# The inverse of a head pair one step earlier in the trace, and three kinds of staging tiles ahead of the merge

## The chip, the cores and the metric

The kernel runs on one core of one Trainium2 chip. The metric is device time in microseconds: the median of three runs is 2133.5 us (2132.93, 2133.5 and 2137.12). A profile is one more execution, taken by the hardware profiler.

## What is computed

One layer of a hybrid encoder on 1024 frames of width 1024, and a final RMSNorm. Cut to what the change touches:

```python
# per head (8 of 128 columns) and chunk, q, k, v after a causal convolution and SiLU
lower = where(strict, beta[..., None] * (k @ k.T) * decay, 0)
sol = triangular_solve(lower, rhs, unit_diagonal=True)     # rhs = [beta*v, beta*exp(gc)*k]
delta = u - w @ state                                      # over the chunks, one after another
o = q_dec @ state + a_qk @ delta
state = g_end * state + k_dec.T @ delta
# then: rmsnorm(o)*silu(z) @ w_branch_gdn, a second branch (GLA) @ w_branch_gla, both merged by gates
```

The rest (GLA branch, cross attention over 256 memory tokens, a squared-ReLU MLP) stands around it unchanged.

## The kernel before

**Precision and products.** A large product is three matmuls of rounded halves, 128x512 each: high by high (L541), high by low (L543), low by high (L545). The halves come from a split: ScalarE rounds to the high half (L581), VectorE or GpSimd subtracts for the low one (L582). The small products of the delta rule are full fp32; each of them stands as two instructions in the trace.

**The delta rule** works on 4 pairs of heads, each head in 8 chunks of 128 frames. For a pair, `push_keys`, and `push_conv` for q and v, queue projections (`dense`, 48 products of 128x512 for each head's q, k or v, followed by three VectorE convolution steps, L1212). `fill(n)` traces n products from that queue, `until(name)` all up to a name. `gdn_keys` makes the triangular matrix NT (L1273, L1276). `gdn_subst` solves its 32x32 diagonal blocks for both heads at once by 62 dependent steps (L1324, L1326) and transposes the result (L1329, L1333). `gdn_inverse` builds the inverse from these blocks in four stages of small matmuls on TensorE (L1356, L1365, L1372, L1379), each of which waits for an eviction by ScalarE or VectorE (L1357 to L1380). `gdn_scan` runs over the chunks: k S and q S (L1404, L1405), zh (L1407, VectorE), NT zh (L1414), dl (L1416, ScalarE), kdt dl (L1421), the new state S (L1424, L1426, VectorE), and AT dl (L1431) for the output v (L1433, L1435). `gdn_norm` (L1450, GpSimd's power at L572, L573 to L576, L1452), `gdn_out` (L1459) and `gdn_sums` (L1469 to L1474) finish a pair in the next round of the loop.

In a round p of the loop (`phase_gdn`) the trace goes: projections of q and v of pair p and k of pair p + 1 are queued; norm and output of pair p - 1; queries and v of pair p; all queued projections to the end; the inverse of pair p; keys and substitution of pair p + 1; the scan of pair p. In the last round (p = 3) no pair follows: after `drain` the pools of the projections are closed, and `begin_merge` opens those of the merge, whose tiles lie where the projections' weights lay.

**The merge's first products.** `begin_merge` fetches weights of the GLA branch (raw, L501 from in_w_bgla_dram, 512 KB each) and loads 20 blocks of 256 KB (obd) of the GLA output, four for each of five operands, through a staging tile `staged`, and splits each into the operand tiles B0a, B0b, A1a, A1b, A0a. All 20 go through the tile "e", which has 3 buffers. The tiles "q" (4 buffers) and "acc" (2) of the same pool are there for later evictions. The products with these operands (pd<-B0a,wop and so on) come later in the trace than the scan of pair 3.

**What sets the order.** The program is traced twice. In the first pass a planner (`Plan`) records every instruction with its tiles, works out dependences and due times from a table of costs, and schedules each engine's list: among instructions whose inputs it holds to be there, TensorE takes the one that was traced first, the other engines the one due first; some sums may go to VectorE or GpSimd. The second pass fixes each engine's order by it. So a place in the trace is a priority, a later product may fill a gap, and the order on the chip is fixed: an instruction that is late holds up all behind it on its engine. SP issues all large transfers, in its own fixed order.

Of the kernel before, what the change touches and what calls it, by code (L numbers as in the profile page):

```python
# [11 lines left out]
F32 = mybir.dt.float32  # L12
# [6 lines left out]
P = 128  # L19
# [8 lines left out]
HALF = 512  # L28
NEG = -1.0e30
NFILL = 4  # L30
GF = (8, 32, 18, 24, 24, 16, 8)
# [117 lines left out]
class Mark:  # L149

    eng, port, dma, flex, acc, cost, lat, own, opcode = "mark", False, False, False, (), 0, 0, 0, ""
# [311 lines left out]
class Layer:  # L463
# [1023 lines left out]
    def phase_gdn(self, wctx):  # L1487

        nc, a = self.nc, self.a
        with ExitStack() as lctx:  # L1490
# [38 lines left out]
            for p in range(GH // 2):  # L1529
                hs = (2 * p, 2 * p + 1)  # L1530
                for h, st in zip(hs, sts):
                    st["q"] = self.til(sq, [P, NB, P], "q", bufs=2)
                    conv(f"q{h}", h, a["w_gdn"][3 * h + 1], lambda acc, st=st: st["q"])
                for h, st in zip(hs, sts):
                    def out(acc, st=st):
                        st["vT"] = c3(acc)
                        return st["vT"]
                    conv(f"v{h}", 2 * GH + h, a["w_gdn"][3 * h + 2], out)
                nxt = None
                if p < GH // 2 - 1:  # L1540
                    nxt = push_keys((2 * p + 2, 2 * p + 3))
                for _ in range(GN[p]):
                    self.push_gate(next(gates), getw, sp)
                if last:
                    for h, st in last:
                        self.gdn_norm(sv, st)
                    self.fill(GF[1])
                    for h, st in last:
                        self.gdn_out(h, st)
                        self.fill(GF[2])  # L1550
                    self.gdn_sums(p - 1, [st for _, st in last])
                else:
                    PF = keys(hs, sts)
                self.until(f"v{hs[0]}")
                self.gdn_queries(sv, sp, sts[0])
                self.fill(GF[3])
                self.gdn_queries(sv, sp, sts[1])
                self.until(f"v{hs[1]}")
                self.gdn_v(sv, sts[0])
                self.fill(GF[4])  # L1560
                self.gdn_v(sv, sts[1])
                self.fill(GF[5])
                if nxt:
                    self.until(f"k{hs[1] + 2}")
                else:
                    self.drain()
                    ectx.close()
                    wctx.close()
                    ob = self.begin_merge()
                self.gdn_inverse(sts, PF, GF[6])  # L1570
                if nxt:
                    ns = (2 * p + 2, 2 * p + 3)
                    for st, h in zip(nxt, ns):
                        self.load_decay(sp, h, st)
                    PF = keys(ns, nxt)
                self.gdn_scan(sv, sq, hs, sts, NFILL)
                for h, st in zip(hs, sts):
                    self.load_z(sv, h, st)
                last, sts = list(zip(hs, sts)), nxt
            sctx.close()  # L1580
            self.big3(ob)
# [10 lines left out]
    def begin_merge(self):  # L1592
# [8 lines left out]
        self.fetch_w()  # L1601
        ob = {"SL": ("B0a", "B0b", "A1a", "A1b", "A0a", "B1a", "B1b")}
        for p in range(5):
            self.load_op(sp, ob, p, lambda p, k: self.obd[p][:, k], range(4), None)
        return ob

    def big3(self, ob):
# [21 lines left out]
    def staged(self, sp, src, both=True):  # L1629

        self.nraw += 1
        raw = self.til(sp, [P, HALF], "e", bufs=3) if both is None or both and self.nraw % 5 < 3 else \
            self.til(self.lp, [P, HALF], "rawa", bufs=2)
        self.load(raw, src)
        return raw
# [978 lines left out]
```

## Time and profile before

| | |
|---|---|
| median of three runs | 2133.5 us |
| profiled execution | 2135.29 us |
| its span, first to last instruction | 2133.6 us |
| TensorE busy | 2105.5 us, 99% |
| VectorE, ScalarE, GpSimd busy | 79%, 53%, 9% |
| mean granted clock of TensorE | 0.994 |
| inverses of the four pairs begin (L1356) | 701.15, 807.34, 913.45, 1008.93 us |
| substitution of pairs 1, 2, 3: first L1315 to last L1333 starts | 734.48 to 786.49, 840.63 to 892.60, 946.73 to 999.90 us |

Times are in microseconds from the span's start. A row of the timeline has the start, the duration, engine, line, operation, output <- inputs, shape and count, and in brackets the idle time before it with what ended it. Busy time of matmuls is modelled, so what TensorE does in a stretch is better read from the starts of its instructions. A granted clock of 0.50 is half speed.

### The profile page before, as it was taken

To read this page: it belongs to the slowest core of one execution; us is meant where nothing else is said; L and a number is where in the kernel's file an instruction comes from. 1 tells how busy PE (TensorE), PEld (TensorE's weight loads), DVE (VectorE), ACT (ScalarE), POOL (GpSimd) and SP (SyncE) were. 2 spreads that over 40 slices of the span, in tenths; PEclk is the share of its full clock that TensorE was granted. 3 is DMA by queue.
4 is the path that set the end of the run, shared out by engine and by line. 5 is a ranking of instruction groups with operands and counts; after the bars stand their busy time and mean duration, and the time that the engine had idled before them with its cause. 6 is when DMAs were issued, how large, how long until landed. Compare 5 with 4: busy or idle time off the path is not lost.

```text
span 2133.6 us, 31820 instructions
## 1 busy us (share of the span) xinstructions
PE 2105.5 (99%) x11340; PEld 1776.2 (83%) x11340; DVE 1688.6 (79%) x3053; ACT 1127.9 (53%) x2251; POOL 182.2 (9%) x194
## 2 busy tenths in 40 slices
PE   8999999999999999999999999999999999999998
PEld 8789888988888888888888888888888888888887
DVE  7869898779768787877799858789979778577766
ACT  6545554454455656565644446676755556444433
POOL 0001101000001121213000001000201000001011
PEclk9999999999999999999899999999999999999999
DMA  8423333223241030302488664457445546688852
GB/s 306 177 80 111 103 112 128 78 87 123 67 147 60 21 114 21 114 11 83 169 300 293 221 197 131 131 183 246 132 138 160 153 148 186 196 273 278 276 178 94
DMA packets 147040, 321.70 MB, mean 151 GB/s; under 512 B 16056, under 2 KB 19512, under 8 KB 146880
## 3 DMA queue, kind: packets, MB, share of 16 engines
q1 hardware_dynamic: 143984, 315.44, 44.5%
q10 hardware_dynamic: 2896, 4.22, 0.6%
q8 instruction: 89, 1.46, 0.3%
q14 instruction: 71, 0.58, 0.1%
HBM read 223.10 MB, written 96.50 MB: 150 GB/s over the span
## 4 chain that ended last, share of the span: by engine, by line
PE 86%; DVE 7%; DMA 3%; ACT 2%; issue 1%; SPq 0%; DVEq 0%; POOLq 0%; ACTq 0%
PE pd L543 20%; PE pd L541 20%; PE pd L545 20%; PE ps L541 5%; PE ps L545 5%; PE ps L543 5%; PE ps L613 2%; DVE acc L1212 1%; DMA raw<-in_w_dram 1%; DVE wop L582 1%; PE ps L1414 1%; PE ps L1421 1%; PE ps L1431 1%; PE ps L1273 1%; ACT wop L581 1%
## 5 line engine op out<-in xcount | busy, mean ns | idle before, releaser
L581 ACT ACTIVATE wop<-raw 128x512 fp32r<-128x512 f32 (+1 forms) x536 | 358.6, 675 | 560.0 <-PE pd L545 263.3
L582 DVE TENSOR_TENSOR wop<-raw,wop 128x512 fp32r<-128x512 f32 (+1 forms) x506 | 370.1, 735 | 116.4 <-ACT wop L581 109.4
L545 PE MATMUL pd<-A1a,wop 128*128 128x512 f32 x380 | 150.0, 395 | 0.0
L541 PE MATMUL pd<-A1a,wop 128*128 128x512 f32 x380 | 148.9, 392 | 0.0
L543 PE MATMUL pd<-A1b,wop 128*128 128x512 f32 x360 | 141.5, 393 | 0.0
L543 PE MATMUL pd<-A1a,wop 128*128 128x512 f32 x316 | 124.4, 394 | 0.2 <-DVE A1a L582 0.2
L545 PE MATMUL pd<-t,wop 128*128 128x512 f32 x300 | 119.3, 398 | 0.0
L541 PE MATMUL pd<-A1b,wop 128*128 128x512 f32 x296 | 117.4, 397 | 1.5 <-ACT A1b L581 1.5
L541 PE MATMUL pd<-t,wop 128*128 128x512 f32 x300 | 116.9, 390 | 0.4 <-ACT wop L581 0.4
L543 PE MATMUL pd<-t,wop 128*128 128x512 f32 x300 | 117.0, 390 | 0.0
L545 PE MATMUL pd<-A1b,wop 128*128 128x512 f32 x296 | 116.8, 395 | 0.0
L1212 DVE SCALAR_TENSOR_TENSOR acc<-cin,convw,acc 128x1024 f32<-128x1024 f32 x72 | 94.3, 1310 | 25.3 <-ACT acc L1210 24.8
L541 PEld LDWEIGHTS pd<-A1a,wop 128*128 128x128 f32 x380 | 71.6, 188 | 14.5
L545 PEld LDWEIGHTS pd<-A1a,wop 128*128 128x128 f32 x380 | 71.5, 188 | 14.0
L541 PE MATMUL pd<-A0a,wop 128*128 128x512 f32 x200 | 81.2, 406 | 0.0
L543 PE MATMUL pd<-A0a,wop 128*128 128x512 f32 x200 | 79.9, 400 | 0.8 <-DVE A0a L582 0.8
L541 PE MATMUL pd<-B0a,wop 128*128 128x512 f32 x196 | 77.7, 397 | 2.6 <-ACT wop L581 2.0
L545 PE MATMUL pd<-A0a,wop 128*128 128x512 f32 x200 | 79.0, 395 | 0.0
L543 PEld LDWEIGHTS pd<-A1b,wop 128*128 128x128 f32 x360 | 67.9, 188 | 13.1
L545 PE MATMUL pd<-B0a,wop 128*128 128x512 f32 x196 | 77.6, 396 | 0.0
L543 PE MATMUL pd<-A0b,wop 128*128 128x512 f32 x188 | 74.8, 398 | 0.0
L545 PE MATMUL pd<-A0b,wop 128*128 128x512 f32 x188 | 74.3, 395 | 0.0
(646 smaller groups left out, 6027.3 us busy)
## 6 DMA issues: line engine op xcount, KB each, us to landing
raw<-in_w_dram SPq DMA_DIRECT2D x120, 256.0 KB, 3.3
raw<-in_w_dram SPq DMA_DIRECT2D x32, 512.0 KB, 4.2
e<-ad SPq DMA_DIRECT2D x63, 256.0 KB, 3.9
raw<-in_w_gdn_dram SPq DMA_DIRECT2D x24, 512.0 KB, 4.2
ad<-q SPq DMA_DIRECT2D x45, 256.0 KB, 2.9
rawa<-ad SPq DMA_DIRECT2D x42, 256.0 KB, 4.5
A0b<-tgd SPq DMA_DIRECT2D x32, 256.0 KB, 5.2
raw<-in_w_gate_dram SPq DMA_DIRECT2D x15, 512.0 KB, 3.6
```

The source lines that it names most:

```text
L541: nc.tensor.matmul(out, lh, rh, start=first and i == 0, stop=False, skip_group_check=more)
L543: nc.tensor.matmul(out, lh, rl, start=False, stop=False, skip_group_check=more)
L545: nc.tensor.matmul(out, ll, rh, start=False, stop=last and i == n - 1, skip_group_check=more)
L581: nc.scalar.activation(hi, raw, AF.Copy)
L582: (lo_eng or nc.gpsimd).tensor_tensor(lo, raw, hi.bitcast(F32), SUB)
L613: self.nc.tensor.transpose(pt[:, i * P:(i + 1) * P], s, self.ident)
L1212: nc.vector.scalar_tensor_tensor(acc, cin[:, 1 + i:1 + i + T], cw[:, i:i + 1], acc, MUL, ADD)
L1273: nc.tensor.matmul(pt[:, i * P:(i + 1) * P], kc, kc, start=True, stop=True)
L1414: nc.tensor.matmul(py[:, 0:P], st["NT"][:, c, :], zh[h], start=True, stop=True)
L1421: nc.tensor.matmul(pd[h][:, 0:P], st["kd"][:, c, :], dl[h], start=True, stop=True)
L1431: nc.tensor.matmul(po[:, 0:P], st["AT"][:, c, :], dl[h], start=True, stop=True)
```

## The change

Two edits. The call of `gdn_inverse` moves: for pair 0 it follows its substitution at once, and for a later pair it is traced right behind the scan of the pair ahead, at the end of that round, and ahead of the next round's queued projections. And the 20 blocks of the merge's first operands go through the tiles q, acc and e in turn (nine buffers) where they went through e alone (three).

```diff
                 else:
-                    PF = keys(hs, sts)
+                    self.gdn_inverse(sts, keys(hs, sts), GF[6])
...
                     ob = self.begin_merge()
-                self.gdn_inverse(sts, PF, GF[6])
                 if nxt:
...
                     self.load_z(sv, h, st)
+                if nxt:
+                    self.gdn_inverse(nxt, PF, GF[6])
                 last, sts = list(zip(hs, sts)), nxt
...
-            self.load_op(sp, ob, p, lambda p, k: self.obd[p][:, k], range(4), None)
+            self.load_op(sp, ob, p, lambda p, k: self.obd[p][:, k], range(4), 3 if p < 5 else None)
...
-        raw = self.til(sp, [P, HALF], "e", bufs=3) if both is None or both and self.nraw % 5 < 3 else \
+        raw = self.til(sp, [P, HALF], *((("e", F32, 3), ("q", F32, 4), ("acc", F32, 2))[self.nraw % 3])) if both == 3 else \
+            self.til(sp, [P, HALF], "e", bufs=3) if both is None or both and self.nraw % 5 < 3 else \
             self.til(self.lp, [P, HALF], "rawa", bufs=2)
```

The planner makes a new order of it. The first place is on TensorE, at the inverse of pair 3: NT_1682 and NT_1704 are the triangular matrices of its two heads, X_9356 and X_9358 the solved blocks and their transposes, pd the bank of a projection. Before the change, from the last projection products on:

```order
L541 MATMUL pd_10119<-A1a_225,wop_10073 128x512
L543 MATMUL pd_10119<-A1a_225,wop_10073 128x512
L545 MATMUL pd_10119<-A1a_225,wop_10074 128x512
L1356 MATMUL ps_10260<-X_9356,NT_1682_9163 32x32 x16
L1356 MATMUL ps_10279<-X_9356,NT_1704_9229 32x32 x16
L1365 MATMUL ps_10298<-X_9358,X_9356 32x32
L1365 MATMUL ps_10298<-X_9356,X_9358 32x32
L1365 MATMUL ps_10298<-X_9358,X_9356 32x32 x2
```

Before the change these L1356 follow the last projection of the gate, and the rows after them hold no other product. After the change the same place of the program, with the same names for pair 3, reads:

```order
L543 MATMUL pd_10100<-A0b_224,wop_10095 128x512
L1356 MATMUL ps_9650<-X_9356,NT_1682_9163 32x32 x16
L1356 MATMUL ps_9669<-X_9356,NT_1704_9229 32x32 x16
L545 MATMUL pd_10100<-A0b_224,wop_10096 128x512
L541 MATMUL pd_10172<-A1b_5434,wop_10095 128x512
L543 MATMUL pd_10172<-A1b_5434,wop_10095 128x512
L545 MATMUL pd_10172<-A1b_5434,wop_10096 128x512
L541 MATMUL pd_10172<-A1a_225,wop_10095 128x512
L543 MATMUL pd_10172<-A1a_225,wop_10095 128x512
L545 MATMUL pd_10172<-A1a_225,wop_10096 128x512
L541 MATMUL pd_10172<-A1b_5434,wop_10095 128x512
L1365 MATMUL ps_9688<-X_9358,X_9356 32x32
```

What moved: before, pd_10119 was the last projection (the gate's), and the first other product came after L1365 of the second head. Now 40 projection products lie between the scan of pair 2 and this inverse, and 8, 18 and 5 between its steps.

The second place is on TensorE, at the start of the scan of pair 3 (v is that scan's zh, dl and S its delta and state, kdt, AT, k and q its keys and queries; pd_10846 and pd_10861 are the merge's first banks). Before the change, in the scan's first chunk:

```order
L1414 MATMUL ps_10404<-v_10059,NT_1682_9163 128x128
L543 MATMUL pd_10846<-B0a_10175,wop_10796 128x512
L545 MATMUL pd_10846<-B0a_10175,wop_10796 128x512
L1414 MATMUL ps_10408<-v_10102,NT_1704_9229 128x128
L1421 MATMUL ps_10412<-dl_10406,kdt_1663_9116 128x128
L541 MATMUL pd_10846<-B0a_10175,wop_10796 128x512
L543 MATMUL pd_10846<-B0a_10175,wop_10796 128x512
L545 MATMUL pd_10846<-B0a_10175,wop_10796 128x512
L541 MATMUL pd_10861<-B0a_10175,wop_10799 128x512
L1421 MATMUL ps_10416<-dl_10410,kdt_1685_9182 128x128
L1431 MATMUL ps_10420<-dl_10406,AT_9908 128x128
L1431 MATMUL ps_10424<-dl_10410,AT_9981 128x128
```

Here the merge's products with B0a stand between the steps of the chunk. After the change the first chunk reads, with pd_10263 the last projection:

```order
L543 MATMUL pd_10263<-A1a_225,wop_10217 128x512
L545 MATMUL pd_10263<-A1a_225,wop_10218 128x512
L1414 MATMUL ps_10404<-v_10203,NT_1682_9163 128x128
L1414 MATMUL ps_10408<-v_10246,NT_1704_9229 128x128
L1421 MATMUL ps_10412<-dl_10406,kdt_1663_9116 128x128
L1421 MATMUL ps_10416<-dl_10410,kdt_1685_9182 128x128
L1431 MATMUL ps_10420<-dl_10406,AT_10052 128x128
L1431 MATMUL ps_10424<-dl_10410,AT_10125 128x128
L1404 MATMUL ps_10428<-S_10414,k_1569_8541 128x128
L1405 MATMUL ps_10428<-S_10414,q_9792 128x128
L1404 MATMUL ps_10435<-S_10418,k_1570_8542 128x128
L1405 MATMUL ps_10435<-S_10418,q_9793 128x128
```

What moved: now the last projection stands right ahead of the scan, the merge's products are gone from its first five chunks (48 products of the scan follow each other), and 32 of them lie in the rest of it, where 66 lay in the whole scan before.

The third place is on VectorE, at the end of the substitution of pair 1 (pr and Pm are its tiles; L1295 belongs to the queries of pair 1, L573 to L576 and L1452 to the norm of pair 0). Before the change the last steps stand together, behind the queries:

```order
L1295 TENSOR_SCALAR eq_7517<-ssq_7490 128x8
L1324 TENSOR_TENSOR pr_6835<-X_6751,Pm_6753 128x70
L1326 TENSOR_TENSOR Pm_6753<-Pm_6753,pr_6835 128x5x14
L1324 TENSOR_TENSOR pr_6838<-X_6751,Pm_6753 128x56
L1326 TENSOR_TENSOR Pm_6753<-Pm_6753,pr_6838 128x4x14
L1324 TENSOR_TENSOR pr_6841<-X_6751,Pm_6753 128x45
L1326 TENSOR_TENSOR Pm_6753<-Pm_6753,pr_6841 128x3x15
L1324 TENSOR_TENSOR pr_6844<-X_6751,Pm_6753 128x30
L1326 TENSOR_TENSOR Pm_6753<-Pm_6753,pr_6844 128x2x15
L1324 TENSOR_TENSOR pr_6847<-X_6751,Pm_6753 128x16
L1326 TENSOR_TENSOR Pm_6753<-Pm_6753,pr_6847 128x16
L1329 STREAM_TRANSPOSE X_6850<-Pm_6753 128x512
```

In these rows only the steps and the queries meet; the norm of pair 0 lies earlier. After the change the last two steps and the transpose read:

```order
L1324 TENSOR_TENSOR pr_6844<-X_6751,Pm_6753 128x30
L575 TENSOR_SCALAR rs_t_7293<-rs_t_7293 128x8
L574 TENSOR_TENSOR rs_t_7304<-rs_t_7304,vv_7301 128x8
L1326 TENSOR_TENSOR Pm_6753<-Pm_6753,pr_6844 128x2x15
L576 TENSOR_TENSOR rs_o_7294<-rs_y_7292,rs_t_7293 128x8
L1324 TENSOR_TENSOR pr_6847<-X_6751,Pm_6753 128x16
L575 TENSOR_SCALAR rs_t_7304<-rs_t_7304 128x8
L1452 TENSOR_TENSOR v_6446<-v_6446,rs_o_7294 128x1024
L1326 TENSOR_TENSOR Pm_6753<-Pm_6753,pr_6847 128x16
L576 TENSOR_TENSOR rs_o_7305<-rs_y_7303,rs_t_7304 128x8
L1329 STREAM_TRANSPOSE X_6850<-Pm_6753 128x512
L1212 SCALAR_TENSOR_TENSOR acc_7513<-cin_7512,convw_212,acc_7513 128x1024
```

What moved: the end of the substitution has moved ahead of the queries of its pair, in between the steps of the norm of pair 0; in the scan of pair 0 its steps now alternate with those of the scan. Of its 248 steps in the program 49 stood on GpSimd before, none now. On SP nine loads of obd now stand ahead of the four weight loads where three stood, and the first of the nine waits for the last projection product; before, the first of the three waited for none.

## The prediction

> **What bounds the kernel now.** I read the page first. TensorE is busy all along, and the chain that ended last is made of it, so a microsecond counts when TensorE has nothing ready or runs at less than its full clock.
>
> ```profile
> span 2133.6 us, 31820 instructions
> PE 2105.5 (99%) x11340; PEld 1776.2 (83%) x11340; DVE 1688.6 (79%) x3053; ACT 1127.9 (53%) x2251; POOL 182.2 (9%) x194
> PE 86%; DVE 7%; DMA 3%; ACT 2%; issue 1%; SPq 0%; DVEq 0%; POOLq 0%; ACTq 0%
> ```
>
> Work is neither added nor dropped on TensorE; only its order changes. So I looked for stretches in which it loses time, by the windows view. First an inverse in the middle (pair 1), then the last one (pair 3) up to the second chunk of its scan, then one chunk of a scan (pair 0). The columns are length, busy time (count) of PE, PEld, DVE, ACT, POOL, granted clock, DMA.
>
> ```profile
> 807.34:820.86 13.52, 12.87 (x247) 10.66 (x246) 8.29 (x11) 9.07 (x18) 0.10 (x1) 1.00 0.14 41
> 1008.92:1030.03 21.11, 17.58 (x248) 15.54 (x248) 10.11 (x20) 12.61 (x27) 0.00 (x0) 0.60 0.51 176
> 1012.66:1029.73 17.07, 14.60 (x132) 12.84 (x133) 8.89 (x17) 9.22 (x19) 0.00 (x0) 0.50 0.46 172
> 743.74:747.03 3.29, 3.29 (x26) 3.03 (x25) 2.94 (x12) 1.94 (x8) 0.50 (x2) 1.00 0.03 5
> ```
>
> The last inverse and one chunk take 21.11 us with about as many matmuls as the middle one has in 13.52 us, and for 17.07 us the granted clock is 0.50. The timeline of TensorE says why: the last projection product (128x512) starts at 1008.61, and until 1018.06 there is nothing but the small matmuls of the inverse, which wait for their own evictions.
>
> ```profile
> 1008.14 0.40 PE L541 MATMUL pd<-A1a,wop 128*128 128x512 f32 x1
> 1008.38 0.39 PE L543 MATMUL pd<-A1a,wop 128*128 128x512 f32 x1
> 1008.61 0.39 PE L545 MATMUL pd<-A1a,wop 128*128 128x512 f32 x1
> 1008.93 1.81 PE L1356 MATMUL ps<-X,NT 32*32 32x32 f32 x58
> ...
> 1013.17 1.94 PE L1372 MATMUL ps<-subTA,NT 64*64 64x64 f32 x16 [1.54 <-DVE subTA L1366]
> ...
> 1018.06 0.80 PE L541 MATMUL pd<-B0a,wop 128*128 128x512 f32 x1 [1.96 <-ACT wop L581]
> ...
> 1030.03 0.39 PE L1404 MATMUL ps<-S,k 128*128 128x128 f32 x2
> ```
>
> **Part 1: the last inverse gets cover.** In the new order the inverse of pair 3 stands behind the scan of pair 2, where projections are left: 8, 18 and 5 of the 128x512 products lie between its steps. What it costs there I take from pair 1, which has 22 such products inside (247 less the inverse's 224 instructions, less an edge). A 128x512 product holds TensorE 0.23 us (1008.14 to 1008.38 to 1008.61), so pair 1's inverse itself takes 13.52 - 22 x 0.23 = 8.4 us. The last one: 21.1 us, less ten 128x512 products (2.3 us), less the six 128x128 products of the scan's first chunk (1.3 us at 0.22 us each, which the next row block shows): 17.5 us. The cover is worth 17.5 - 8.4 = **9.1 us**.
>
> **Part 2: the scan of pair 3 loses its cover.** With the inverse gone from there, the first five chunks of that scan stand bare: 48 products of 128x128 without one of 128x512 between them. The price comes from one chunk of pair 0, all engines:
>
> ```profile
> 743.74 0.39 PE L1404 MATMUL ps<-S,k 128*128 128x128 f32 x2
> 743.96 0.39 PE L1405 MATMUL ps<-S,q 128*128 128x128 f32 x2
> 744.39 0.35 DVE L1407 SCALAR_TENSOR_TENSOR zh<-ps,geg,v 128x128 f32<-128x128 f32 x1
> 744.87 0.42 PE L1414 MATMUL ps<-zh,NT 128*128 128x128 f32 x2
> 744.87 0.72 ACT L1409 ACTIVATE qs<-ps,geg 128x128 f32<-128x128 f32 x2
> 745.49 0.72 ACT L1416 ACTIVATE dl<-ps,nb 128x128 f32<-128x128 f32 x2
> 746.05 0.70 PE L1421 MATMUL ps<-dl,kdt 128*128 128x128 f32 x4
> 746.47 0.80 DVE L1426 SCALAR_TENSOR_TENSOR S<-S,gge,ps 128x128 f32<-128x128 f32 x2
> ```
>
> A 128x128 product is two instructions, 0.22 us (743.74 to 743.96). A chunk has ten, 2.2 us, and takes 3.29 us; four 128x512 products (0.92 us) fill all but 0.17 us of the rest. The 3.29 us are the chain k S, zh, NT zh, dl, kdt dl, S. Bare, the chunk loses the 0.92 us if the chain keeps its length. ScalarE's new order has the first dl ahead of the second qs, half of 0.72 us earlier: then it is 0.56 us. I take 0.75 us, four times, 3.0 us. The first chunk has only the hops, from start to start, L1414 to L1416 (0.62), to L1421 (0.56), to L1426 (0.42), to L1404 (747.03, 0.56): 2.16 us, less six products, 0.8 us. In the fifth chunk three splits of the staged operands stand on ScalarE ahead of its dl: each takes at least as long as a 128x128 step (0.36 us), 1.1 us in all, and most of it fits into ScalarE's idle time (1.94 of 3.29 us are busy); I add 0.4 us, an estimate. Sum **4.2 us**, between 2.6 (four times 0.56, and 0.4) and 5.6 (four times 0.92, 0.8 and 1.1).
>
> Whether the clock holds there is the second question. What bears on it are stretches of about 3.4 us, three from early in the kernel and two from the last inverse, in the same view as above:
>
> ```profile
> 63.75:67.17 3.42, 2.35 (x9) 1.21 (x8) 3.42 (x7) 0.89 (x2) 0.88 (x1) 1.00 0.02 5
> 67.17:70.58 3.41, 1.16 (x8) 0.97 (x8) 2.16 (x6) 0.81 (x2) 0.00 (x0) 1.00 0.62 192
> 70.58:74.00 3.42, 3.21 (x8) 2.54 (x9) 3.38 (x7) 2.00 (x4) 0.00 (x0) 0.50 0.10 38
> 1009.25:1012.66 3.41, 2.35 (x108) 2.07 (x102) 0.91 (x3) 3.18 (x9) 0.00 (x0) 1.00 0.86 227
> 1012.66:1016.07 3.41, 2.90 (x64) 2.71 (x64) 0.78 (x2) 2.36 (x6) 0.00 (x0) 0.50 0.89 339
> ```
>
> With TensorE busy 2.35 of 3.42 us on whole 128-row products the clock stays at 1.00; after 1.16 of 3.41 us it is 0.50; and after 2.35 of 3.41 us on 32x32 tiles (the row at 1009.25) it is 0.50 as well. The bare scan is busy 2.2 of 3.0 to 3.3 us on whole products, nearest to the first row, so I take no loss. [...]
>
> **Part 3: the substitution gets a date.** The inverse of pairs 1 to 3 now waits for the substitution (L1324, L1326), which VectorE does during the scan ahead; until now it had the whole next round of projections as slack.
>
> ```profile
> 759.60 0.16 DVE L1450 SCALAR_TENSOR_TENSOR vv<-ss,eq 128x8 f32<-128x8 f32 x1
> ...
> 761.55 0.17 DVE L573 TENSOR_TENSOR rs_t<-rs_y 128x8 f32<-128x8 f32 x1 [1.46 <-POOL rs_y L572]
> ...
> 763.16 0.17 DVE L573 TENSOR_TENSOR rs_t<-rs_y 128x8 f32<-128x8 f32 x1 [1.24 <-POOL rs_y L572]
> ...
> 763.64 1.23 DVE L1452 TENSOR_TENSOR v<-v,rs_o 128x1024 f32<-128x1024 f32 x1
> L1324 DVE TENSOR_TENSOR pr<-X,Pm 128x126 f32<-128x126 f32 (+21 forms) x105 | 26.7, 254 | 2.6
> L1326 DVE TENSOR_TENSOR Pm<-Pm,pr 128x110 f32<-128x110 f32 (+13 forms) x94 | 23.7, 252 | 2.4
> L1329 DVE STREAM_TRANSPOSE X<-Pm x4: 1057/1081/1091, 682.8 to 996.1; 128x512 f32<-128x512 f32 x4
> ```
>
> In the new order 12 steps, the norm of the pair ahead and the transpose L1329 stand behind the scan's last v: 12 x 0.25 = 3.0, two waits for GpSimd of some 1.2 = 2.4, L1452 1.2, eight tiny ones some 0.8, L1329 1.1, together 8.5 us and a hop or two. TensorE has 40 products of 0.23 us = 9.2 us before the inverse. So the margin is about nil: I take 0.3 us of waiting per pair, **0.9 us**, between 0 and 3. What runs late next is the inverse, and behind it in TensorE's queue the projections of the next pair.
>
> **Part 4: the staging.** Nine loads of the merge's operands now stand in SP's queue ahead of the four of its weights, the first of them waiting for the last projection product; until now it was three, one of them free of that wait.
>
> ```profile
> 1003.54 6.05 SPq L501 DMA_DIRECT2D e<-obd  x3
> 1010.11 2.31 SPq L501 DMA_DIRECT2D raw<-in_w_bgla_dram  x4
> e<-obd SPq DMA_DIRECT2D x21, 256.0 KB, 2.9
> raw<-in_w_bgla_dram SPq DMA_DIRECT2D x4, 512.0 KB, 7.3
> ```
>
> The first product that needs the weights started at 1018.06, 9.5 us behind the last projection product's start. Two of the three loads were issued behind that product too; now nine are, seven more of 256 KB, 1.8 MB. At the 339 GB/s of the row at 1012.66 that is 5.4 us more, at the 227 GB/s of the row before it 8.1 us: 14.9 to 17.6 us. The bare chunks cover 2.2 + 4 x 3.2 = 15.0 us and two products and the scan's start some 0.6 more. So the edit costs nothing by itself at the faster rate, which held while only loads ran, and I take **0**; at the slower one 2.0 us of waiting. It gains nothing either: what it brings earlier is needed behind the scan. The tiles q and acc are used next by the evictions of those very products (L1781), later.
>
> **The sum.** -9.1 + 4.2 + 0.9 = -4.0 us, on the profiled execution 2135.29 to 2131.3 us. That execution is 1.7 us above its span and 1.8 us above the median of the three runs, 2133.5 us, so I forecast 2133.5 - 4.0 = **2129.5 us**. By the bounds of parts 2 to 4 it reaches from 9.1 - 2.6 = 6.5 us gained to 9.1 - 5.6 - 3.0 - 2.0 = 1.5 us lost. A measurement of this kernel can tell about 0.2%, 4.3 us, from no change; my forecast lies just inside that.
>
> **The rivals.** *More is gained.* The other inverses get more cover too, 31 products for 22. What they can give is their waiting at L1372, 6.6 us in all seven cases with the 1.54 of the last pair:
>
> ```profile
>   DVE subTA L1366: 6.6, 7
> ```
>
> With some 4 us of that gone the time is 2125.5. Against it: the new order fits the cover to the step that follows, as the old one did. Chance 0.15.
>
> *VectorE becomes the bound in the scans (slower).*
>
> ```profile
> L1212 DVE SCALAR_TENSOR_TENSOR acc<-cin,convw,acc 128x1024 f32<-128x1024 f32 x72 | 94.3, 1310 | 25.3 <-ACT acc L1210 24.8
> ```
>
> Where it decides: a chunk of the scans of pairs 0 to 2 now holds up to nine projection products, 2.2 + 9 x 0.23 = 4.3 us of TensorE, and VectorE holds the same 12 instructions as in the row at 743.74 (2.94 us) and in many chunks a convolution step of 1.3 us, 4.2 us together; 49 of the substitution's 248 steps, which stood on GpSimd, stand on VectorE now as well. If VectorE needs over 4.3 us, each chunk and the inverse behind it come late by the rest: at 0.6 us in 21 chunks 12.6 us, giving 2142. For it: two orders interleaved instruction by instruction, so each S and zh of the scan's chain can stand behind a step. Against it: VectorE was at 2.94 of 3.29 us before without holding TensorE up. Chance 0.14.
>
> *The clock falls in the bare scan.* At half clock the ten products take 4.4 us for 3.2: 4 x 1.2, 0.5 in the first chunk, and some 1.2 until it is back, 6.5 us, giving 2136. The rows at 63.75 and 1009.25 have the same busy time and went either way. [...] Chance 0.08.
>
> *Nothing comes of it.* The 128x512 products that no longer lie in the scan of pair 3 follow it and wait there for the staged operands instead: the gain goes back, 2133.5. For it: 32 of them lie in that scan, 66 before. Against it: their operands are asked for earlier. Chance 0.08.
>
> **How the numbers follow.** The forecast's case keeps 0.55; about half of its width, 0.30, is over 4.3 us. Faster 0.30 + 0.15 = 0.45; slower 0.14; the same 0.41. The range takes in parts 2 and 3, most of the first rival and the second half-way: 2124 to 2140.
>
> **What would show it.** Right: the granted clock stays at 1.00 from the last projection to the end of pair 3's scan; five chunks of that scan some 3 us apart with TensorE idle 0.6 to 0.9 us in each; TensorE's wait for X at L1356 under 1 us per pair; no wait of a 128x512 product for wop or B0a beyond 1 us. Wrong: clock 0.50 in the scan, chunks over 4.3 us apart in pairs 0 to 2, or idle time ahead of L1356.

## The result, and the profile after

The changed kernel takes 2149.55 us (median of four runs, 2148.99 to 2152.25); the kernel before, on the same chip, 2135.31 us (2132.93 to 2137.35). The ratio is 1.0072, with a 95% interval of 1.006 to 1.0084: it is slower, by some 15 us, where 4.0 us of gain were forecast and 2140 was the upper end of the range. (Ratios here and below are of undisturbed runs alone, so they can differ a little from the quotient of the medians.)

The head of the page of the kernel after shows no more work: TensorE has the same 11340 matmuls, 8 us more of busy time and a span that is 14.7 us longer.

```profile
span 2148.3 us, 31801 instructions
PE 2113.9 (98%) x11340; PEld 1777.1 (83%) x11340; DVE 1699.9 (79%) x3097; ACT 1126.8 (52%) x2251; POOL 178.4 (8%) x150
```

TensorE's waits in the kernel after: what it waited for, in total, how often, the longest.

```profile
PE ps L1356 <- DVE X L1329: 6.1, 4, 2.5
...
PE pd L541 <- ACT wop L581: 2.8, 3, 2.2
PE pd L541 <- DVE u L1825: 2.2, 1, 2.2
```

The wait of the inverse (L1356) for the substitution (X, L1329) is on top, four times; the kernel before has no such row. Two waits of 2.2 us come from quite another place (wop are the halves of a weight, u is a partial sum in the MLP). (Line numbers from L1577 on are up to two higher than before.) Where the time went is best read in three pieces between instructions that mark the same place in both programs: the last L1076, the second chunk of the scan of pair 3 (L1404), the first L1835 (L1837 after) in the MLP, and the first L2402 (L2404), the last product but one. First the kernel before, in rows of single lines (their times are first and last start); the fourth mark, 1030.03, is a row of the prediction:

```profile
L1076 PE MATMUL ps<-S,qk x56: 379/379/483, 209.9 to 559.3; 128*128 128x256 f32 x56
L1835 ACT ACTIVATE u<-pd x4: 589/598/600, 1845.6 to 1848.3; 128x512 f32<-128x512 f32 x4
L2402 PE MATMUL pd<-dg,A0b x32: 272/275/276, 2119.9 to 2124.7; 128*128 128x128 f32 x32
```

and the kernel after:

```profile
L1076 PE MATMUL ps<-S,qk x56: 379/379/483, 209.0 to 558.4; 128*128 128x256 f32 x56
1030.52 0.39 PE L1404 MATMUL ps<-S,k 128*128 128x128 f32 x2
L1837 ACT ACTIVATE u<-pd x4: 580/594/601, 1852.7 to 1855.3; 128x512 f32<-128x512 f32 x4
L2404 PE MATMUL pd<-dg,A0b x32: 272/275/275, 2134.7 to 2139.5; 128*128 128x128 f32 x32
```

Before, ten of the merge's products (2.3 us) were done by 1030.03, after none, so 2.3 us are taken off the first piece of before and put on its second. Then:

| piece | before | after | difference |
|---|---|---|---|
| delta rule, up to the second chunk of the last scan | 468.5 | 472.1 | +3.6 |
| the rest of that scan, the merge and what follows, up to the MLP | 817.8 | 822.2 | +4.4 |
| the MLP's last product | 274.3 | 282.0 | +7.7 |

The sum is 15.7 us (1.0 us of it is not in the span, since the kernel after started that much faster). The forecast for the three was -7.4 (-9.1, +0.9 and the 0.8 of the first bare chunk), +3.4 and 0. The second is near, though it holds all that happens up to the MLP and not the bare scan alone; the first and the third are far off.

**The first piece.** The timeline of all engines at the end of the substitution of pair 3, in the kernel after:

```profile
988.04 2.39 POOL L582 TENSOR_TENSOR wop<-raw,wop 128x1024 fp32r<-128x1024 f32 x1
988.11 2.35 DVE L573 TENSOR_TENSOR rs_t<-rs_y 128x8 f32<-128x8 f32 x1 [1.23 <-POOL rs_y L572]
...
992.34 1.03 DVE L1329 STREAM_TRANSPOSE X<-Pm 128x512 f32<-128x512 f32 x1
...
993.43 1.29 PE L1356 MATMUL ps<-X,NT 32*32 32x32 f32 x39 [1.25 <-DVE X L1329]
```

The same of pair 0:

```profile
671.96 0.21 DVE L1324 TENSOR_TENSOR pr<-X,Pm 128x45 f32<-128x45 f32 x1
672.00 2.41 POOL L582 TENSOR_TENSOR wop<-raw,wop 128x1024 fp32r<-128x1024 f32 x1 [4.65 <-ACT wop L581]
672.20 2.27 DVE L1326 TENSOR_TENSOR Pm<-Pm,pr 128x45 f32<-128x45 f32 x1
...
676.47 1.98 PE L1356 MATMUL ps<-X,NT 32*32 32x32 f32 x64 [2.47 <-DVE X L1329]
```

An L573 on 128x8 took 0.17 us here in the kernel before; now it takes 2.35 us, and no wait for that is recorded (the 1.23 us in brackets are its wait for L572, which the kernel before has too): it starts 0.07 us behind a subtraction on GpSimd of 2.39 us, the low half of a projection's weights, and ends 0.03 us behind it. In pair 0 an L1326 of some 0.2 us does the same. Pairs 1 and 2 show the L573 of pair 3 again (2.35 and 2.34 us). L1329 and the inverse are late by that much, and TensorE has used up its 40 products.

What such a wait costs is more than its length. The windows view of the kernel after, in pairs 1, 2 and 3 two neighbouring stretches of 3.41 us each, the first with the wait in it; the columns are length, busy time (count) of PE, PEld, DVE, ACT, POOL, granted clock, DMA.

```profile
773.03:776.44 3.41, 2.20 (x17) 1.51 (x18) 3.41 (x13) 0.00 (x0) 0.40 (x2) 1.00 0.00 0
776.44:779.86 3.42, 3.42 (x71) 3.07 (x67) 3.36 (x5) 1.84 (x5) 3.42 (x2) 1.00 0.00 0
882.25:885.67 3.42, 2.22 (x58) 1.76 (x58) 3.42 (x6) 0.38 (x1) 1.50 (x1) 1.00 0.00 0
885.67:889.08 3.41, 3.41 (x25) 2.76 (x20) 3.35 (x4) 2.48 (x7) 3.35 (x3) 0.50 0.02 5
991.48:994.89 3.41, 2.16 (x56) 1.70 (x56) 3.41 (x6) 0.34 (x1) 1.45 (x1) 1.00 0.01 2
994.89:998.31 3.42, 3.42 (x27) 2.77 (x22) 3.36 (x4) 2.48 (x7) 3.36 (x3) 0.50 0.02 5
```

Three waits of 1.20 to 1.25 us, and in pairs 2 and 3 the clock falls to half for the next 3.41 us, in pair 1 it doesn't: its stretch ends 0.2 us behind the wait and has only 17 matmuls, about half of them of 128x512, while those of pairs 2 and 3 go on for 1.5 us and have most of their 58 and 56 matmuls in 32x32 tiles. In pair 0 it is half for 6.8 us. The run e8 below has the same order up to the MLP and the same wait in pair 1 (1.25 us), and there the clock did fall, for 3.4 us: whether it falls is not settled by the wait alone.

**The second piece.** The bare scan, as forecast at full clock; the windows are the short first chunk of pair 3 (from its L1414) and the four whole chunks behind it, from L1404 to L1404, in the kernel after.

```profile
1028.38:1030.52 2.14, 1.64 (x13) 1.44 (x12) 0.50 (x3) 1.11 (x3) 0.00 (x0) 1.00 0.32 116
1030.52:1033.87 3.35, 3.25 (x22) 2.53 (x21) 1.78 (x7) 1.92 (x8) 0.00 (x0) 1.00 0.97 293
1033.87:1037.22 3.35, 3.25 (x22) 2.53 (x21) 1.86 (x7) 1.85 (x8) 0.00 (x0) 1.00 0.89 270
1037.22:1040.57 3.35, 3.25 (x22) 2.53 (x21) 1.86 (x7) 2.68 (x10) 0.00 (x0) 1.00 1.05 421
1040.57:1044.28 3.71, 2.84 (x23) 2.46 (x22) 3.39 (x10) 3.39 (x12) 0.00 (x0) 1.00 0.87 342
```

Three chunks of 3.35 us and one of 3.71 (in which the splits of the staged operands stand), where 2.2 us are the issue of matmuls: 3 x 1.15 + 1.5 = 5.0 us without a product, and 2.14 - 1.32 = 0.8 in the first chunk.

**The third piece.** In the last product of the MLP, 900 us behind anything that the diff touches, the timeline of the kernel after has this:

```profile
2060.70 4.25 POOL L582 TENSOR_TENSOR wop<-raw,wop 128x512 fp32r<-128x512 f32 x3 [78.54 <-ACT wop L581]
2062.33 3.16 DVE L1830 TENSOR_TENSOR A0b<-acc,A0b 128x512 f32<-128x512 f32 x2
...
2066.75 0.79 PE L541 MATMUL pd<-t,wop 128*128 128x512 f32 x1 [2.17 <-DVE u L1825]
```

The same sum in the kernel before (L1828 there; shortest, median and longest in ns):

```profile
L1828 DVE TENSOR_TENSOR A0b<-acc,A0b x3: 678/684/989, 2050.3 to 2063.3; 128x512 f32<-128x512 f32 x3
```

Again subtractions on GpSimd, again a VectorE sum that takes 1.6 us (3.16 for two) in place of 0.68, again a wait of TensorE, with 3.4 us at half clock behind it. A second wait of 2.18 us, for weights (wop, L581) at 1964.08, has 3.4 us at half clock behind it as well.

### The profile page after: what moved, and what is told of

Same layout as the page of the kernel before. It is cut to its first block, busy times and chain, and to the rows that moved or that the text cites. A ratio compares the mean times of both kernels' runs of the same rounds, so it can differ in the third digit from the quotient of the medians.

```text
span 2148.3 us, 31801 instructions
## 1 busy us (share of the span) xinstructions
PE 2113.9 (98%) x11340; PEld 1777.1 (83%) x11340; DVE 1699.9 (79%) x3097; ACT 1126.8 (52%) x2251; POOL 178.4 (8%) x150
## 4 chain that ended last, share of the span: by engine, by line
PE 37%; DVE 7%; DMA 4%; issue 1%; ACT 1%; SPq 0%; POOL 0%; DVEq 0%; POOLq 0%; ACTq 0%
PE pd L543 8%; PE pd L541 8%; PE pd L545 8%; PE ps L545 4%; PE ps L541 4%; PE ps L543 4%; DVE wop L582 1%; DMA raw<-in_w_dram 1%; DMA A0b<-tgd 1%; DMA e<-ad 1%; DMA rawa<-ad 0%; DMA raw<-ald 0%; DVE q L1783 0%; DVE u L1783 0%; PE ps L613 0%
## 5 line engine op out<-in xcount | busy, mean ns | idle before, releaser
L581 ACT ACTIVATE wop<-raw 128x512 fp32r<-128x512 f32 (+1 forms) x536 | 358.4, 674 | 531.5 <-PE pd L545 265.4
L543 PEld LDWEIGHTS pd<-A1b,wop 128*128 128x128 f32 x360 | 68.1, 189 | 13.7 <-DVE A1b L582 0.2
```

Source lines behind the costliest of these rows:

```text
L543: nc.tensor.matmul(out, lh, rl, start=False, stop=False, skip_group_check=more)
L581: nc.scalar.activation(hi, raw, AF.Copy)
```

## The experiments

The theory after the result: **the moved inverse has too little slack for what GpSimd holds up.** One split on GpSimd beside the end of the chain makes it 2.3 us late, TensorE waits and its clock falls. Rival A: the chain (12 steps, norm, transpose) is too long for 40 products, whatever GpSimd does. Rival B: the staging edit is at fault, not the inverse. Each run has the ratio to the kernel before with its interval, and the three pieces as differences to before, worked out as above from one profiled execution; one period of half clock (3.4 us) more or less moves a piece by up to half of that, 1.7 us.

| run | inverse moved | staging | splits on VectorE | ratio | pieces 1, 2, 3 |
|---|---|---|---|---|---|
| changed kernel | all | q, acc, e | none | 1.0072 (1.006 to 1.0084) | +3.6, +4.4, +7.7 |
| e1 | all | old | none | 1.0064 (1.0051 to 1.0078) | +3.9, +9.7, -1.4 |
| e2 | none | q, acc, e | none | 1.0034 (1.0022 to 1.0046) | -2.3, -1.6, +11.5 |
| e3 | all | q, acc, e | projections | 1.0038 (1.0023 to 1.0053) | -4.0, +4.4, +6.0 |
| e4 | pairs 1 to 3, later | old | none | 1.003 (1.002 to 1.0041) | -4.3, +9.8, -1.3 |
| e5 | all | q, acc, e | delta rule and last product | 1.0019 (1.001 to 1.0029) | -6.4, +4.2, +8.5 |
| e6 | pair 3 | q, acc, e | delta rule and last product | 1.0046 (1.0034 to 1.0059) | +1.3, +7.2, +1.7 |
| e7 | none | old | delta rule and last product | 1.0004 (0.9995 to 1.0014) | -1.5, -0.2, +1.0 |
| e8 | all | q, acc, e | last product | 1.0069 (1.0053 to 1.0085) | +4.3, +4.4, +3.9 |
| e9 | all | acc, e, q | delta rule | 1.003 (1.002 to 1.0041) | -7.9, +10.2, +3.4 |
| e10 | all | q, acc, e for 16 blocks | delta rule | 1.0019 (1.001 to 1.0028) | -6.4, +6.6, +1.8 |
| e11 | all | acc, e, q | none | 1.0077 (1.0065 to 1.0089) | +4.3, +9.6, +3.1 |
| e12 | all | e, q, q | delta rule | 1.0035 (1.0022 to 1.0049) | -7.9, +7.6, +4.9 |

### The two edits apart (e1, e2)

e1 keeps the old staging:

```diff
-            self.load_op(sp, ob, p, lambda p, k: self.obd[p][:, k], range(4), 3 if p < 5 else None)
+            self.load_op(sp, ob, p, lambda p, k: self.obd[p][:, k], range(4), None)
```

> The inverse moved, the staging as before (tile e alone). All theories: the waits ahead of L1356 (6.1 us in the changed kernel) and the halved clock behind them stay, so up to the scan of pair 3 it reads as the changed kernel, some 9 us late before the last inverse and 4 to 8 us late behind that scan. Of the 7.7 us that the changed kernel loses in the last 200 us (two waits of 2.2 us on TensorE, each with 3.4 us at half clock): if the staging edit brought them through the planner's order, they are gone and the time is some 2142; if the moved inverse brought them, they stay and it is some 2149.

2146.57 us, above the 2142 that were expected if the staging brought the late waits. The first piece is the changed kernel's (+3.9), with 6.2 us of waits ahead of L1356. The late waits are gone (-1.4). But the second piece is 5.3 us worse than the changed kernel's, which nobody expected. In e1's timeline the operand that follows the new ones, B1a, is waited for, and its clock falls to 0.50 right behind, for 3.4 us:

```profile
1080.76 1.26 ACT L581 ACTIVATE B1a<-e 128x512 fp32r<-128x512 f32 x2 [1.05 <-DMA e<-obd]
1081.44 0.73 PE L541 MATMUL pd<-B1a,wop 128*128 128x512 f32 x2 [0.84 <-ACT B1a L581]
1083.07 0.53 PE L543 MATMUL pd<-B1a,wop 128*128 128x512 f32 x1 [0.89 <-DVE B1a L582]
```

So with the inverse out of the way the merge comes early enough to run into its own loads, and the changed kernel with its nine buffers has no such wait. e2 is the other edit alone, in the kernel before:

```diff
-            self.load_op(sp, ob, p, lambda p, k: self.obd[p][:, k], range(4), None)
+            self.load_op(sp, ob, p, lambda p, k: self.obd[p][:, k], range(4), 3 if p < 5 else None)
...
-        raw = self.til(sp, [P, HALF], "e", bufs=3) if both is None or both and self.nraw % 5 < 3 else \
+        raw = self.til(sp, [P, HALF], *((("e", F32, 3), ("q", F32, 4), ("acc", F32, 2))[self.nraw % 3])) if both == 3 else \
+            self.til(sp, [P, HALF], "e", bufs=3) if both is None or both and self.nraw % 5 < 3 else \
```

> The staging changed, the inverse where it was before. Up to the merge nothing changes under any theory: no wait ahead of L1356, the last inverse at half clock. If the staging edit brings the late waits through the planner's order, the last 200 us lose some 7 us and the time is 2140 to 2142; if they came with the moved inverse, it is within 2 us of before. If the staging edit gained by itself (loads earlier), it would show as faster products behind the last inverse, 1 to 2 us.

2141.19 us, ratio 1.0034: near the 2140 to 2142 that were expected if the late loss is the staging's. The first two pieces gain 3.9 us, the last product loses 11.5 us, with a wait of 3.2 us for u and one of 2.4 us for wop, and two periods of half clock. No e-run with the old staging (e1, e4, e7) loses over 1.0 us there; every one with a new staging loses 1.7 to 11.5. The wait for u (2.2 to 3.2 us) stands in six of the seven kernels that have a new staging and leave the last product's splits free (all but e10, which waits 2.5 us for wop instead), and in none with the old staging. Rival B is right on the third piece and wrong on the first.

### The splits off GpSimd (e3, e5, e7, e8)

e3 fixes the low halves of the projections' weights on VectorE, in the changed kernel; `self.tc.nc` goes past the planner's choice.

```diff
-            w = self.wpart(src, [NB, P])
+            w = self.wpart(src, [NB, P], self.tc.nc.vector)
             cw = self.convw[:, blk, :]
```

> The changed kernel, with the low halves of the delta rule's projection weights (L582, 128x1024) fixed on VectorE, so that none of them runs on GpSimd beside the end of the substitution. Theory (GpSimd's split of 2.4 us holds up one VectorE instruction of 0.2 us for its whole length): no L1326 or L573 of 2.3 us is left, the wait ahead of L1356 falls from 1.2 to 2.5 us a pair to under 0.5, the clock stays at 1.00 there, and the stage is 8 to 12 us shorter: 2138 to 2141. Rival (the chain of substitution, norm and transpose is too long for 40 products, whatever GpSimd does): waits and clock stay, 2148 to 2150, or more since VectorE has three or four splits of 1.1 us more.

2143.0 us, 2 us above the 2138 to 2141 of the theory and below the 2148 to 2150 of the rival. Pair 2 of e3, in the timeline:

```profile
874.77 0.17 DVE L573 TENSOR_TENSOR rs_t<-rs_y 128x8 f32<-128x8 f32 x1 [1.39 <-POOL rs_y L572]
874.93 1.23 DVE L582 TENSOR_TENSOR wop<-raw,wop 128x1024 fp32r<-128x1024 f32 x1
...
876.38 0.17 DVE L573 TENSOR_TENSOR rs_t<-rs_y 128x8 f32<-128x8 f32 x1
...
880.08 1.13 PE L1356 MATMUL ps<-X,NT 32*32 32x32 f32 x34
```

No held instruction and no wait for X, though VectorE does the split itself (1.23 us) in the middle of the chain: rival A falls. The clock stays at 1.00 in pairs 0 to 2. Pair 3 is a control that wasn't planned: its round has a gate projection, whose split comes from another line and stayed on GpSimd, and it alone still has the held instruction, the wait, and 6.8 us at half clock.

```profile
982.71 2.39 POOL L582 TENSOR_TENSOR wop<-raw,wop 128x1024 fp32r<-128x1024 f32 x1
982.78 2.35 DVE L573 TENSOR_TENSOR rs_t<-rs_y 128x8 f32<-128x8 f32 x1 [1.23 <-POOL rs_y L572]
...
986.60 1.98 PE L1356 MATMUL ps<-X,NT 32*32 32x32 f32 x64 [1.18 <-DVE rs_o L576]
```

e5 fixes that one too, and the splits of the last product's weights, in two lines of the MLP (e8 has only these two):

```diff
-            getw = lambda src: self.wpart(src, [NB, P])
+            getw = lambda src: self.wpart(src, [NB, P], self.tc.nc.vector)
...
-                self.split(w, t[:, 0], t[:, 1], nc.vector if len(ps) == 2 or k % 2 else None)
+                self.split(w, t[:, 0], t[:, 1], self.tc.nc.vector)
...
-                    self.split(raw, t[:, 0], t[:, 1])
+                    self.split(raw, t[:, 0], t[:, 1], self.tc.nc.vector)
```

> The changed kernel with all low halves of the delta rule's weights on VectorE (the projections and now the gate too), and those of the last product's weights (two lines of the MLP) as well. Theory: in the run before with only the projections fixed, the one pair whose gate split was left on GpSimd (pair 3) kept the held instruction of 2.35 us, the wait of 1.2 us and 6.8 us at half clock; here it goes too, so no clock of 0.50 is left between 600 and 2100 us, the wait of 2 to 3 us for u near the end goes, and the time is 2127 to 2132, below before. Rival (pair 3 waits because its round has more work, or the late wait is a transfer's): 2138 to 2143 as with the projections alone.

2139.97 us, above the 2127 to 2132 of the theory and inside the rival's 2138 to 2143. The first piece decides between them for pair 3: it did what was expected, -6.4 us, 10.0 us better than the changed kernel. One period of half clock is left of those that were to go, in pair 0; from 681 to 2100 us there is none. The two stretches around its start, and the inverse of pair 3 from its first L1356 to the matmul behind its last L1379, in e5:

```profile
674.16:677.57 3.41, 2.99 (x69) 2.68 (x69) 3.34 (x5) 1.81 (x5) 2.92 (x2) 1.00 0.00 0
677.57:680.99 3.42, 3.42 (x55) 2.48 (x54) 3.32 (x5) 2.52 (x7) 0.17 (x1) 0.50 0.02 5
985.88:997.78 11.90, 11.73 (x243) 9.73 (x242) 8.28 (x11) 7.30 (x17) 1.03 (x1) 1.00 0.01 3
```

In pair 0 of e5 TensorE waits 0.43 us for X, and yet the clock falls behind a stretch in which 64 of 69 matmuls are 32x32 tiles.

The last piece went the other way, +8.5: with the splits on VectorE no wait there is over 1.5 us, but there are several, two for wop (1.48 and 1.45 us) and three for u (1.8 us in all). e7 puts the same fixes into the kernel before.

> The kernel before with the same splits fixed on VectorE and nothing else: the control. Theory: there the substitution has a round of slack, so nothing that GpSimd holds up is waited for; within 2 us of before, with the last inverse at half clock as before. If it gains over 3 us, the gain of the other two versions is the split's and not the inverse's.

2135.9 us, ratio 1.0004 with 1 inside the interval: without the moved inverse the splits' engine makes no difference that could be measured. So the 10 us are the two together. e8 is the changed kernel with the last product's two lines alone.

> The changed kernel with only the low halves of the last product's weights (the MLP) on VectorE. Theory: everything up to 1900 us stays as in the changed kernel, 7 to 8 us behind before; of the two late waits the one for u (GpSimd's three splits of 128x512 beside the evictions, 4.0 us with its clock) goes; 2143 to 2146. Rival (the late loss has to do with transfers or the planner's order elsewhere): it stays at 2148 to 2150.

2149.68 us, missed: the third piece falls from +7.7 to +3.9, and the half clock there is gone, but the time stays; pieces one and two read as the changed kernel's within 0.7 us, but the profiled execution of e8 is 2.4 us later at the last L1076, ahead of any edit, which takes up most of the gain. Its six timed runs lie 6 us apart, and the changed kernel's four 3 us, so they can't tell such a gain from none. What GpSimd holds up is about half of the late loss by one profile, and not shown by the timed runs.

### Where the inverse stands (e4, e6)

e4 is the kernel before with the inverse of pairs 1 to 3 traced behind the norm, output and sums of the pair ahead; the staging stays the old one:

```diff
                     self.gdn_sums(p - 1, [st for _, st in last])
+                    self.gdn_inverse(sts, PF, GF[6])
                 else:
...
-                self.gdn_inverse(sts, PF, GF[6])
+                if p == 0:
+                    self.gdn_inverse(sts, PF, GF[6])
```

> The inverse of pairs 1 to 3 traced behind the norm, output and sums of the pair ahead, a third of a round later than in the changed kernel and still ahead of the last projections; staging and pair 0 as before. Theory: the inverse of pair 3 keeps its cover (9 us gained), the substitution has some 68 products more before its date, so no wait ahead of L1356 and no clock of 0.50; the bare scan of pair 3 costs some 4 to 6 us. Up to the merge 3 to 5 us ahead of before; the planner's order of the last 200 us adds anything from 0 to 8 us. 2129 to 2137. Rival (the cover of the last inverse is worth less than the bare scan costs): not ahead of before behind the scan of pair 3.

2139.64 us, above the 2129 to 2137 that were expected. One wait ahead of L1356 is left (1.0 us, pair 1, with 6.8 us at half clock), and the first piece gains 4.3 us, as expected. The second loses 9.8, as in e1, for the same wait for B1a at 1075 and 1080 us: the time that the last inverse gains is given back to the loads of the merge. e6 moves the inverse of pair 3 alone, with the new staging and the fixed splits (the diff shows the move alone, against the kernel before).

```diff
-                self.gdn_inverse(sts, PF, GF[6])
+                if p < 3:
+                    self.gdn_inverse(sts, PF, GF[6])
...
+                if p == 2:
+                    self.gdn_inverse(nxt, PF, GF[6])
```

> Only the inverse of pair 3 is traced behind the scan ahead, those of pairs 0 to 2 where they were; the new staging; the same splits fixed on VectorE. Theory: moving pairs 0 to 2 gains nothing (their inverses were covered), so this keeps the gain of the last inverse (9 us), pays the bare scan (3.6 us) and has the gain of the staging behind it (2 us): 2125 to 2129, no slower than the version with all pairs moved. Rival (the other pairs' additional cover is worth something): 1 to 3 us behind that version.

2145.54 us, far from 2125 to 2129. In this order the inverse of pair 2 has lost its cover: its products wait 2.09 us for weights (920.53, wop L581), and the clock is at half for 17.1 us, as it was in pair 3 before.

```profile
919.50:936.60 17.10, 16.07 (x139) 13.98 (x140) 6.44 (x11) 6.86 (x20) 0.62 (x2) 0.50 0.11 32
```

Which of e6's edits did that wasn't tried.

### The late loss (e9 to e12)

Is the third piece an accident of the planner's order? Four runs change which of the tiles the loads take, and in what turn. e9 and e11 differ in the delta rule's splits alone; e10 and e12 are two more orders with these splits fixed. The lines are shortened to the part that differs:

```diff
-*((("e", F32, 3), ("q", F32, 4), ("acc", F32, 2))[self.nraw % 3])
+*((("acc", F32, 2), ("e", F32, 3), ("q", F32, 4))[self.nraw % 3])      # e9 and e11
+*((("e", F32, 3), ("q", F32, 4), ("q", F32, 4))[self.nraw % 3])        # e12
-range(4), 3 if p < 5 else None)
+range(4), 3 if p < 4 else None)                                        # e10
```

> The delta rule's weight splits (projections and gate) fixed on VectorE, the inverse moved, and the same three staging tiles taken in another turn (acc, e, q instead of q, acc, e); the last product's splits are free again. Up to 1900 us it should read as the version with all splits fixed, 2 to 3 us ahead of before. Theory: the 7.7 us that the changed kernel loses behind 1940 us are an accident of the planner's order (the order of its SP loads there comes out nearer to the kernel with the old staging now), so they go or shrink: 2129 to 2134. Rival (the loss hangs on the staging's nine tiles themselves): behind 1940 us 7 to 8 us as before, 2138 to 2142.

> The changed kernel with nothing else than the other turn of the staging tiles (acc, e, q). Up to 1900 us as the changed kernel, 7 to 8 us behind before: GpSimd's splits, the waits ahead of L1356 and the halved clock stay. Behind it the accident of the planner's order: if it is one, 2140 to 2144; if the staging itself costs there, 2148 to 2150. The difference to the run with the same turn and fixed splits is the price of GpSimd's splits beside the substitution: by theory 9 to 11 us.

> As the run with the turned staging, but with the turn of the changed kernel, and only the first 16 of the 20 blocks over three tiles (the last four, A0a, through e alone). Same theories: up to 1900 us 2 to 3 us ahead of before; behind it, if the loss is an accident of the order, some value between -1.5 and 8 us that has nothing to do with the number of tiles; 2129 to 2140.

> As the run with 16 blocks, but with all 20 blocks over two kinds of tiles, e and twice q (seven buffers), splits of the delta rule fixed on VectorE. Up to the end of the scan of pair 3 (1060 us) it should read as the other runs with fixed splits, 1.7 to 3.3 us ahead of before from the same start. Behind it, if seven buffers are enough, no wait for loads at 1080 us (with three buffers 7.4 us), and behind 1940 us a loss between -1.5 and 8 us. 2130 to 2139; below 2132 it would beat both kernels.

2141.57, 2150.51, 2138.57 and 2140.05 us: e10 is inside its range, e12 1 us above; e9 and e11 missed the range that they had for an accident of the order (2129 to 2134, 2140 to 2144) and lie in or just above the one for a cost of the staging itself (2138 to 2142, 2148 to 2150). In e11 the turn alone more than halves the late loss (7.7 to 3.1), but the second piece grows by 5.2, to 9.6; e9 has 3.4 and 10.2 (e5, with 8.5 and 4.2, differs from it in the last product's splits too): e9 waits 1.96 us for B0a at 1199.27, with 3.4 us at half clock behind it, e11 1.95 us at 1213.34 without, e12 2.94 us for B0b at 1201.22. So the loss is not tied to one place: it moves between the two pieces, and none of the eight runs with an inverse moved and a new staging stays below +8 us in the two together. Some 5 us of that are the bare scan itself, and with the old staging e1 and e4 come to 8.3 and 8.5 as well. e9 against e11 prices the splits once more: 12.2 us in the first piece, 8.9 us in the timed medians.

Over all runs the first piece falls into two groups: inverse moved with the splits free, +3.6 to +4.3 (the changed kernel, e1, e8, e11); moved with the delta rule's splits fixed, -6.4 to -7.9 (e5, e9, e10, e12). No run beats the kernel before; of those with an inverse moved, e5 and e10 come nearest (1.0019).

## Why the prediction was wrong

**What bounds it, and part 1 (the last inverse, 9.1 us).** Right. In e5 the inverse of pair 3 takes 11.90 us with 17 products of 128x512 in it (243 matmuls less 224, less two behind it): 8.0 us, against 17.5 before, 9.5 us gained. In the changed kernel half clock ate a part of it.

**Part 2 (the bare scan, 4.2 us, between 2.6 and 5.6).** Right in its mechanism and a little low: chunks of 3.35 us where 3.2 were taken; 5.0 + 0.8 = 5.8 us of TensorE's time, of which 0.8 lie in the first piece. Less the 0.17 us that the prediction left in a covered chunk too, four times, it is 5.1 us by its own measure, inside its bounds; the second, with all that follows up to the MLP, is 4.4 us longer than before. The clock stayed at 1.00 through the bare scan in the changed kernel and in every run with all inverses moved: the rival of the falling clock there fell.

**Part 3 (the date of the substitution, 0.9 us, between 0 and 3).** This is the step that failed: 0.9 us were taken, and the first piece came out at +3.6 us where -7.4 were forecast, 11.0 us later. The margin was right, nil; in e3, with GpSimd out of the way, pairs 1 and 2 don't wait. The durations were wrong: the sum took each VectorE instruction as long as in the kernel before, and left out what the new order puts beside it on GpSimd. The prediction counted the 49 substitution steps that left GpSimd as load for VectorE, and never asked what GpSimd does in their stead; its splits of 128x1024 went from three to five, and four of them start 3 to 5 us ahead of an L1329. What a wait costs was wrong too: 6.1 us of waiting came with 13.7 us at half clock, and with a margin of nil the upper end had to hold that. And pair 0 was not priced at all: its inverse moved as well, and has the longest wait, 2.47 us. With the delta rule's splits fixed the first piece is at -6.4 to -7.9 us in four runs, where the forecast had it: what the step lacked was GpSimd.

What was missed stands in the trace of the kernel before too, away from the inverses: one of its 28 L573, on 128x8 at 342.99 us, took 1.04 us in place of 0.17; it started 0.08 us behind an L1223 of 1.10 us on GpSimd and ended 0.02 us behind it. In the kernel after it is 2.35 us in place of 0.17 beside 2.39 us on GpSimd. It should have been a rival. Not every VectorE instruction beside GpSimd is held (an L1229 on 128x8 took 0.20 us at 341.33, inside an L572 of 1.65 us), and by what the held ones are picked no run here shows.

On the clock, the windows at 991.48 and 882.25 agree with those of the prediction: some 2.2 us of busy time that is mostly 32x32 tiles, and the clock falls. The periods of half clock have a common measure: 3.41 us (the row at 885.67), 6.8 us (pair 0 of the kernel after), 13.7 us (e2, from 1012.2) and 17.1 us (the kernel before, and e6) are one, two, four and five times 3.41 us, within 0.1 us. A fall needs no long gap ahead of it: the longest in pairs 2 and 3 was 1.25 us, and in pair 0 of e5 it was 0.43 us. What sets the fall off is not shown by these runs.

**Part 4 (the staging, 0).** Wrong twice. It looked at the first operands only; the next one, B1a, is where the loads fall short once the inverse is out of the way, and there the edit is worth 5.3 us (e1 against the changed kernel), though not in every order: with the same nine buffers in another turn (e11) the second piece is 9.6 us again, by a wait for B0a. And with it the last product loses 7.7 us (11.5 in e2, where it is the only edit), a stage that the prediction never looked at, though the order of it was to be had beforehand. What there decides stays open: by the profile GpSimd's splits are in it (e8), and the tiles that the loads take (e9 to e12 move it), but no run removed it with a new staging.

**The rivals.** "More is gained": TensorE's waits at L1372 did shrink, from 6.6 us to 2.3 in e5, but with the splits fixed the first piece shows nothing like 4 us beyond the forecast. That VectorE becomes the bound in the scans of pairs 0 to 2 is refuted: the first piece would not be 6 to 8 us ahead in e5 and e9, where VectorE has more to do still. The kernel did become slower, as that rival said, but not by its mechanism. "Nothing comes of it" had the right idea for e1 and e4, where waits for the loaded operands take gain back. None of the rivals had GpSimd holding up VectorE.

## What to carry to other kernels

When a chain is given a date, list what the other engines run beside its last few microseconds in the new order, GpSimd first: a sum of durations from another order holds only for that order. With TensorE at 99%, a wait of 1.2 us that is followed by 3.4 us at half clock costs some 2.9 us (1.2 and half of 3.4, an estimate), so a margin of nil isn't a margin. And where a planner orders the whole program, compare the orders of all stages, not of the edited one: here half of the loss lay 900 us behind the edit.

## What the hardware showed that was not expected

A held instruction shows no wait of its own in these profiles: its duration grows (L573 0.17 to 2.35 us, L1326 some 0.2 to 2.27, the sum at L1828, L1830 after, 0.68 to 1.6), so it is found by comparing durations of one form, not in the waits. The same wait of 1.2 us halves the clock in one place and execution and not in another: in the changed kernel it did in pairs 2 and 3 and not in pair 1, in e8, with the same order, in pair 1 too. And the fall needs no wait of that length: 0.43 us went ahead of it in pair 0 of e5, behind 64 matmuls of 32x32.
